# Moving one scale of the first tile from VectorE to ScalarE in a row normalization

## The chip, the cores and the metric

The kernel runs on one core of one Trainium2 chip. The metric is device time in microseconds (us) of one execution. Six runs of the kernel before and six of the changed one were taken in turn; a profile of one execution of each is read beside them. All runs are at a granted clock of 1.0.

## The reference

Each of 1024 rows of 4096 fp32 numbers is divided by its Euclidean norm.

```python
def reference(x, axis, eps):            # x: [1024, 4096] fp32, axis -1, eps 1e-12
    norm = np.sqrt(np.sum(x ** 2, axis=axis, keepdims=True) + eps)
    return (x / norm).astype(np.float32)
```

Every element is read once and written once: 16.78 MB in, 16.78 MB out.

## The kernel before

There are two tiles. A tile holds 512 rows: 128 partitions with R = 4 rows of 4096 elements each, 64 KB per partition and 8.39 MB in all. Both loads are issued at the start, on SyncE's DMA queue. For each tile, VectorE squares and sums row 3, ScalarE squares and sums rows 0, 1 and 2; ScalarE takes the root, VectorE the reciprocal; VectorE scales all four rows in place. Then one store sends the tile out on the same queue.

```python
    def scale(self, r):
        self.nc.vector.tensor_scalar_mul(
            out=self.x[:, r], in0=self.x[:, r], scalar1=self.rstd[:, r : r + 1]
        )
# ... (pools, constants)
    for i in range(n_tiles):
        g = RowGroups(nc, io, stats, scratch, D, R, eps_t)
        load = nc.sync.dma_start(out=g.flat(), in_=x_t[i])
        # ...
    for i, g in enumerate(groups):
        g.square_dve(R - 1)
        g.square_act(0)
        g.norm(0)
        g.scale(0)
        g.square_act(1)
        g.norm(1)
        g.norm(R - 1)
        g.scale(1)
        g.scale(R - 1)
        g.square_act(2)
        g.norm(2)
        g.scale(2)
        store = nc.sync.dma_start(out=out_t[i], in_=g.flat())
```

## Time and profile before

| | before |
|---|---|
| time, median of the first 3 runs | 82.73 us (82.72 to 83.13) |
| time, median of all 6 runs of the comparison | 82.97 us (82.72 to 83.13) |
| span of the profile | 81.1 us |
| VectorE / ScalarE busy | 28.6 us (35%) / 26.4 us (33%) |
| DMA queue, share of 16 engines' span | 97.1% |
| store 0 issued / tile 1's squares start / store 1 issued | 37.88 / 41.91 / 57.27 us |

Two rows of the groups of instructions matter for the change: the second holds the scale that moves, and the first ScalarE's squares, from which the length of the new Copy can be judged. The columns are line, engine, operation, output and input with shapes and count; then busy us and the mean ns of one; then the idle time before them and what ended it.

```profile
L33 ACT ACTIVATE sq_act<-xt 128x4096 f32<-128x4096 f32 x6 | 21.6, 3608 | 26.5 <-DMA xt<-in_x_dram 26.5
L64 DVE TENSOR_SCALAR xt<-xt,rstd 128x4096 f32<-128x4096 f32 x8 | 18.8, 2353 | 0.3
```

Until their last instructions the engines are idle mostly because they wait for loads (26.5 us on ScalarE, 25.0 us on VectorE). The queue row and the windows that the prediction shows say the same from the other side: the DMA engines are what is full.

### The profile page before, as it was taken

How to read it: one execution, taken by the hardware profiler on the slowest of the kernel's cores; microseconds unless marked ns; L12 is line 12 of the kernel's file. 1: busy time of each engine (PE TensorE's matmuls, PEld its weight loads, DVE VectorE, ACT ScalarE, POOL GpSimd, SP SyncE). 2: the span in 40 equal slices, each digit the busy share in tenths (PEclk: the TensorE clock that was granted, in tenths of full speed). 3: DMA queues.
4: the chain of work that ended last, by engine and by line, in shares of the span. 5: the costliest groups of instructions: out<-in, count | busy, mean ns of one | idle time of the engine just before them, and what ended most of it. 6: DMA issues, size and time to landing. Idle time of an engine off the chain costs nothing.

```text
span 81.1 us, 93 instructions
## 1 busy us (share of the span) xinstructions
DVE 28.6 (35%) x21; ACT 26.4 (33%) x22; POOL 0.2 (0%) x4
## 2 busy tenths in 40 slices
DVE  0000000000199599976039995999200000000000
ACT  6000000000199999930039999950000000000000
POOL 0000000000000000000000000000000000000000
DMA  9099999299999759999099995899998399998390
GB/s 517 0 517 517 517 517 485 129 420 517 517 517 485 323 226 517 517 517 517 0 517 517 517 452 226 355 517 517 517 485 388 162 517 517 517 517 388 162 485 0
DMA packets 577, 33.55 MB, mean 414 GB/s; under 512 B 65, under 2 KB 65, under 8 KB 65
## 3 DMA queue, kind: packets, MB, share of 16 engines
q1 hardware_dynamic: 576, 33.55, 97.1%
q14 instruction: 1, 0.00, 0.0%
HBM read 16.78 MB, written 16.78 MB: 414 GB/s over the span
## 4 chain that ended last, share of the span: by engine, by line
DMA 51%; ACT 10%; DVE 9%; issue 0%
DMA xt<-in_x_dram 51%; ACT sq_act L33 9%; DVE xt L64 9%; ACT rstd L53 1%; DVE rstd L59 0%
## 5 line engine op out<-in xcount | busy, mean ns | idle before, releaser
L33 ACT ACTIVATE sq_act<-xt 128x4096 f32<-128x4096 f32 x6 | 21.6, 3608 | 26.5 <-DMA xt<-in_x_dram 26.5
L64 DVE TENSOR_SCALAR xt<-xt,rstd 128x4096 f32<-128x4096 f32 x8 | 18.8, 2353 | 0.3
L42 DVE SCALAR_TENSOR_TENSOR sq_dve<-xt 128x4096 f32<-128x4096 f32 x2 | 8.9, 4426 | 25.0 <-DMA xt<-in_x_dram 25.0
L53 ACT ACTIVATE rstd<-ssq,eps_t 128x1 f32<-128x1 f32 x8 | 2.1, 288 | 0.1
L59 DVE RECIPROCAL rstd<-rstd 128x1 f32<-128x1 f32 x8 | 1.3, 159 | 2.4 <-ACT rstd L53 2.4
L33 ACT ACT_TABLE_LOAD x1 | 1.3, 1283 | 0.8 <-PEq L220 0.8
L53 ACT ACT_TABLE_LOAD x1 | 1.3, 1283 | 0.0
L33 ACT ACTIVATION_READ_ACCUMULATOR sq_act<-xt 128x1 f32 x6 | 1.1, 186 | 0.0
L176 DVE MEMSET eps_t<- 128x1 f32 x1 | 0.1, 59 | 0.9 <-PEq L220 0.9
L42 DVE DVE_READ_ACCUMULATOR sq_dve<-xt 128x1 f32 x2 | 0.2, 83 | 0.0
L220 POOL MEMSET const-uint8-127<- 128x1 uint8 x1 | 0.1, 102 | 0.0
L220 POOL MEMSET const-bfloat16-1.0<- 128x1 bf16 x1 | 0.1, 101 | 0.0
L220 POOL MEMSET const-float32-0.0<- 128x1 f32 x1 | 0.1, 98 | 0.2 <-issue 0.2
L220 POOL MEMSET const-float32-1.0<- 128x1 f32 x1 | 0.1, 98 | 0.0
## 6 DMA issues: line engine op xcount, KB each, us to landing
xt<-in_x_dram SPq DMA_DIRECT2D x2, 31.5
out_dram<-xt SPq DMA_DIRECT2D x2, 23.3
```

Source lines behind the costliest of these rows:

```text
L33: self.nc.scalar.activation(out=sq_a, in_=self.x[:, r], func=ACT_F.Square, accum_out=self.ssq[:, r : r + 1],)
L42: self.nc.vector.scalar_tensor_tensor(out=sq_v, in0=self.x[:, r], scalar=1.0, in1=self.x[:, r], op0=ALU.mult, op1=ALU.mult, accum_out=self ...
L53: self.nc.scalar.activation(out=self.rstd[:, r : r + n], in_=self.ssq[:, r : r + n], func=ACT_F.Sqrt, bias=self.eps_t,)
L59: self.nc.vector.reciprocal(out=self.rstd[:, r : r + n], in_=self.rstd[:, r : r + n])
L64: self.nc.vector.tensor_scalar_mul(out=self.x[:, r], in0=self.x[:, r], scalar1=self.rstd[:, r : r + 1])
L176: nc.vector.memset(eps_t, eps)
L220: nc = _bacc.Bacc("TRN2", target_bir_lowering=False, num_devices=1)
```

## The change

The intent is to relieve VectorE at the end of tile 0: its last scale there becomes a Copy with a per-row scale on ScalarE, which has nothing else to do until load 1 lands. Tile 1 is left alone, because there the last scale is followed by the last store and VectorE is the quicker engine.

```diff
+    def scale_act(self, r):
+        self.nc.scalar.activation(
+            out=self.x[:, r],
+            in_=self.x[:, r],
+            func=ACT_F.Copy,
+            scale=self.rstd[:, r : r + 1],
+        )
 ...
-        g.scale(2)
+        if i < n_tiles - 1:
+            g.scale_act(2)
+        else:
+            g.scale(2)
         store = nc.sync.dma_start(out=out_t[i], in_=g.flat())
```

## The prediction

> **What bounds the kernel now.** I read the busy table first: VectorE (DVE) is busy 35% of the span and ScalarE (ACT) 33%, so neither engine fills it. The slices, the packet line and the queue row come next.
>
> ```profile
> DMA  9099999299999759999099995899998399998390
> ...
> DMA packets 577, 33.55 MB, mean 414 GB/s; under 512 B 65, under 2 KB 65, under 8 KB 65
> ...
> q1 hardware_dynamic: 576, 33.55, 97.1%
> ```
>
> The one queue that carries both loads and both stores occupies the 16 DMA engines for 97.1% of the span. The single 0s between 9s in the slices are no holes: a packet is booked, with its bytes and its whole time, where it starts, and all 16 engines start their packets almost together. Each of the four transfers is 8.39 MB, 128 packets of 64 KB, so eight per engine. The windows of busy time, cut to fit the rounds of packets, show how long one lasts (DMA share times the length of the window, for 16 packets) and when it starts (columns: window, length, DVE, ACT, POOL, clock, DMA share, GB/s):
>
> ```profile
> 1.00:1.60 0.60, 0.00 (x0) 0.60 (x1) 0.00 (x0) 1.00 5.17 1748
> ...
> 35.60:36.10 0.50, 0.50 (x1) 0.00 (x0) 0.00 (x0) 1.00 4.88 2097
> 36.10:38.00 1.90, 1.75 (x1) 0.00 (x0) 0.00 (x0) 1.00 0.00 0
> 38.00:38.50 0.50, 0.00 (x0) 0.00 (x0) 0.00 (x0) 1.00 5.84 2097
> 38.50:40.80 2.30, 0.00 (x0) 0.00 (x0) 0.00 (x0) 1.00 0.00 0
> 40.80:41.60 0.80, 0.00 (x0) 0.00 (x0) 0.00 (x0) 1.00 2.84 1229
> ```
>
> 2097 GB/s for 0.50 us is 1.05 MB, 16 packets. A packet of the next to last load round took 4.88 x 0.50 = 2.44 us; the very first round took 5.17 x 0.60 = 3.10 us[...]. The last load round starts in 38.00 to 38.50 and takes 5.84 x 0.50 = 2.92 us, so it ends near 41.2 on average, and there the next 16 packets start (1229 GB/s for 0.80 us is 15 of them). Those are the first packets of store 0. The engines have no hole at this hand-over; only that last load round is 0.5 us longer than the usual 2.42, a fact I come back to. Four transfers of eight rounds are 32 x 2.42 = 77.4 us; with 1.0 us until the first packet, 0.7 us extra in the first round, 0.5 us at the hand-over, 0.1 us elsewhere and roughly 1 us for receipts and the closing barrier this gives the 81.1 us of the span. Bandwidth, not arithmetic, sets the end.
>
> The timeline shows when store 0 was ready, and the DMA queue's own waits what it stood behind:
>
> ```profile
> 34.98 0.29 ACT L53 ACTIVATE rstd<-ssq,eps_t 128x1 f32<-128x1 f32 x1
> 35.30 0.16 DVE L59 RECIPROCAL rstd<-rstd 128x1 f32<-128x1 f32 x1 [0.57 <-ACT rstd L53]
> 35.50 2.35 DVE L64 TENSOR_SCALAR xt<-xt,rstd 128x4096 f32<-128x4096 f32 x1
> 37.88 0.35 SPq L202 DMA_DIRECT2D out_dram<-xt  x1
> 41.91 3.62 ACT L33 ACTIVATE sq_act<-xt 128x4096 f32<-128x4096 f32 x1 [6.64 <-DMA xt<-in_x_dram]
> 41.91 4.43 DVE L42 SCALAR_TENSOR_TENSOR sq_dve<-xt 128x4096 f32<-128x4096 f32 x1 [4.06 <-DMA xt<-in_x_dram]
> ...
> SPq L202 <- DVE xt L64: 31.3, 2, 15.9
> SPq L234 <- DMA out_dram<-xt: 22.5, 2, 19.3
> ```
>
> The scale to be changed is the row at 35.50. Store 0 is issued at 37.88, but its packets start only from 40.8 on. Both compute engines then sit idle until 41.91, when load 1 has landed. The queue waits up to 15.9 us for the scales, yet the DMA engines are never empty meanwhile: such a wait is one of the issuing queue, not of the transfers. The chain of work that ended last, as printed, stops at the last scale (54.89); the 23 us after it are store 0's rest and store 1.
>
> **What the Trainium skill says.** ScalarE: Activation LUTs, section What ACT_TABLE_LOAD costs: an ACTIVATE with immediate scale and bias takes 186 ns plus 0.833 ns per element, and each [128,1] operand adds about 93 ns. The trace agrees: the squares of 4096 elements mean 3608 ns, the formula 3598. The same page, section Table sets: cheap functions, copy among them, are in every set, so Copy between Sqrt and Square should switch no table; in the trace Square already follows Sqrt without a second switch, and the changed program's list of ScalarE instructions has no added load. VectorE: DVE Perf Modes, section The perf-mode tier table: fp32 tensor_scalar from SBUF runs at twice the base rate; the trace has 2353 ns for 4096 elements, 1.74 elements per ns, so it does. DMA: Bandwidth & Descriptors, section Queues, rings and completion order: on each DMA engine descriptors are consumed in ring order. Store 0 starting only as load 1's last round ends agrees.
>
> **The change part by part.** The listing of both programs' instructions says: on VectorE one scale of tile 0 goes and nothing else moves; on ScalarE one Copy comes between the last square root of tile 0 and the first square of tile 1; on the queue, store 0 now waits for ScalarE. Tile 1 keeps all its work.
>
> Removed: 2.35 us of VectorE (35.50 to 37.85). Behind it VectorE has only the wait until 41.91, so this frees nothing: its idle time before tile 1 grows from 4.06 to about 6.6 us.
>
> Added: one ACTIVATE of 4096 elements with a [128,1] scale. My estimate from the skill's figures is 3598 + 93 = 3.69 us; from the measured squares it would be at least 3.60. ScalarE is free from 35.27, but the reciprocal it needs ends at 35.46, so it starts at about 35.50 and ends at about 39.19. ScalarE's next work starts at 41.91, so 2.7 us remain and no tile 1 work is pushed.
>
> Moved: the issue of store 0. Before, it came 0.03 us after the scale's end (35.50 + 2.35 = 37.85, issue at 37.88). Now it is 39.19 + 0.03 = 39.22, which is 1.34 us later.
>
> What that is worth depends on the hand-over. Load 0 was issued at 0.00 and its first packets started in 1.0 to 1.6, so I take 1.0 to 1.6 us from issue to first packet. Store 0's packets could then start at 40.2 to 40.8. Before, the engines came free for them from about 40.8 to 41.6. So the later issue still comes some 0.6 to 0.8 us ahead, where it was about 2 us ahead. On the path: 0. In the sum: minus 2.35 off the path, plus 3.69 off the path, 1.34 later into a slack of about 2.0. The load of tile 1, its arithmetic and the issue of store 1 at 57.27 stay where they are, and store 1 again waits in its ring behind store 0, which goes on until near 60.5.
>
> **The rivals.** *Rival 1: the slack is not there.* The last load round is 0.5 us long already. If this comes from store 0's descriptors arriving too late for the engines to look ahead to, the issue time is on the path now, and a delay of 1.34 us goes through partly or wholly: up to 82.73 + 1.34 = 84.07 us, 1.6% more. Even if the engines want the descriptors only one path filling (3.10 - 2.42 = 0.68 us) ahead of the data, then 0.6 to 0.8 us of lead is just enough, and without the long round, with engines free from 40.5, a few tenths would show. Against it speaks the hand-over from store 0 to store 1: store 1 is issued at 57.27, its descriptors arrive at 58.3 to 58.9, when the last round of store 0 is already running (it starts in 57.7 to 58.5), and that round is not longer (3.02 x 0.80 = 2.42 us for 16 packets). The long round may so belong to turning from loads to stores. I give 20% to a loss of 0.1 to 0.7 us and 12% to one nearer 1.3.
>
> *Rival 2: VectorE's relief helps.* Its idle time turns into an earlier end only if something of tile 1 could start earlier. Both first squares of tile 1 wait for the load at 41.91, so this yields 0, 82.7 us. Some gain could come only from the hand-over itself: if a later issue takes the extra 0.5 us out of the last load round, 82.3 us. I give 5% to that.
>
> *Rival 3: ScalarE becomes the bound.* It would have to be busy past 41.91, that is, the Copy would have to last 6.4 us, or switch tables twice (2 x 1.28 us, the rows of its table loads) and still end at 41.8. Neither fits the list of instructions; it would cost a few tenths at most, 83 us.
>
> **Range and chances.** The most likely result is no change, 82.73, with run-to-run scatter of 82.72 to 83.13 in the runs before. Weighing 63% at about 0, 20% at +0.4, 12% at +1.3 and 5% at -0.4 gives +0.2; the middle of the outcomes lies nearer zero, so I say 82.85 us. The range of 82.4 to 83.9 leaves out the corner of each rival. Faster by 2% would need 1.65 us, more than the hand-over has to give; slower by 2% would need 1.65 us also, above the full 1.34. Chances: faster 0.01, same 0.96, slower 0.03.
>
> **What would show each step.** Right: a Copy row of 3.6 to 3.7 us on ScalarE at 35.5, store 0 issued near 39.2, tile 1's squares still at 41.9 and the queue's share still near 97%. The hand-over is settled by when store 0's first packets start: 40.8 to 41.6 as before means hidden. If they start later by most of 1.34 us, or the last load round grows beyond 2.92 us, the slack step was wrong. A table load beside the Copy, or tile 1's squares later than 41.9, would make the ScalarE step wrong.

## The result, and the profile after

| | before | after |
|---|---|---|
| median of 6 runs | 82.97 us (82.72 to 83.13) | 82.53 us (82.44 to 82.70) |
| ratio after / before | | 0.9953 (95% interval 0.9930 to 0.9975) |

A ratio here is the mean time of one kernel's runs over the mean of the other's of the same rounds, so it is not quite the ratio of the medians. As predicted, 82.53 lies in the range. But the interval excludes 1: the kernel is 0.44 us faster by the medians, although the prediction said that nothing on the path would move.

The page of the kernel after, its packet line, its queue row and the row of the new instruction:

```profile
DMA packets 576, 33.55 MB, mean 416 GB/s; under 512 B 64, under 2 KB 64, under 8 KB 64
...
q1 hardware_dynamic: 576, 33.55, 97.0%
...
L69 ACT ACTIVATE xt<-xt,rstd 128x4096 f32<-128x4096 f32 x1 | 3.7, 3708 | 0.2 <-DVE rstd L59 0.2
```

The same bytes, the same share of the queue, a little more GB/s, and a Copy of 3708 ns without a table load. The timeline of the kernel after (start us, length us, engine, line, operation; idle time before it and what ended it in brackets):

```profile
35.48 3.71 ACT L69 ACTIVATE xt<-xt,rstd 128x4096 f32<-128x4096 f32 x1 [0.23 <-DVE rstd L59]
39.21 17.74 SPq L213 DMA_DIRECT2D out_dram<-xt  x2
41.25 3.62 ACT L33 ACTIVATE sq_act<-xt 128x4096 f32<-128x4096 f32 x1 [2.06 <-DMA xt<-in_x_dram]
41.25 4.43 DVE L42 SCALAR_TENSOR_TENSOR sq_dve<-xt 128x4096 f32<-128x4096 f32 x1 [5.81 <-DMA xt<-in_x_dram]
```

Store 0 is issued 1.33 us later (39.21 against 37.88), as worked out (1.34). Yet load 1 has landed 0.66 us *earlier* (41.25 against 41.91), and nothing in the change touches the load. The windows of the kernel after, cut at the rounds of packets, show where this comes from (columns: window, length, VectorE, ScalarE and GpSimd busy, clock, DMA share, GB/s; the share times the length is the mean time of a packet when all 16 start in the window):

```profile
35.50:36.10 0.60, 0.00 (x0) 0.60 (x1) 0.00 (x0) 1.00 4.03 1748
...
37.90:38.50 0.60, 0.00 (x0) 0.60 (x1) 0.00 (x0) 1.00 4.03 1748
38.50:40.50 2.00, 0.00 (x0) 0.69 (x1) 0.00 (x0) 1.00 0.00 0
40.50:41.05 0.55, 0.00 (x0) 0.00 (x0) 0.00 (x0) 1.00 4.47 1907
```

The last load round (37.90 to 38.50) takes 4.03 x 0.60 = 2.42 us, the usual length, where it took 2.92 before. The next 16 packets, store 0's first, start from 40.5 on. By the single packet records each engine now stands empty for 0.10 to 0.25 us, 0.18 us on average, between its last load packet and its first store packet; before there was no such hole.

The sum, from the packet records averaged over the 16 engines: the last load round is 0.50 us shorter; the three rounds before it, which were 0.13 us too long in the profile of before, are normal; the first round began and ran 0.10 us later; the hole costs 0.18 us; the 16 store rounds are together 0.13 us longer. That is -0.50 - 0.13 + 0.10 + 0.18 + 0.13 = -0.22 us. The end is set by the slowest of the 16 engines, not by the mean. The ends of the last packets lay 0.74 us apart before and lie 0.48 us apart after, so the slowest ends 0.43 us earlier (79.80 against 80.23), and the span falls from 81.1 to 80.7.

### The profile page after: what moved, and what is told of

It is laid out like the page before. It is cut to its first block, busy times and chain, and to the rows that moved or that the text cites. A ratio compares the mean times of both kernels' runs of the same rounds, so it can differ in the third digit from the quotient of the medians.

```text
span 80.7 us, 93 instructions
## 1 busy us (share of the span) xinstructions
DVE 26.2 (33%) x20; ACT 30.1 (37%) x23; POOL 0.2 (0%) x4
## 4 chain that ended last, share of the span: by engine, by line
DMA 50%; ACT 10%; DVE 9%; issue 0%
DMA xt<-in_x_dram 50%; ACT sq_act L33 9%; DVE xt L64 9%; ACT rstd L53 1%; DVE rstd L59 0%
## 5 line engine op out<-in xcount | busy, mean ns | idle before, releaser
L64 DVE TENSOR_SCALAR xt<-xt,rstd 128x4096 f32<-128x4096 f32 x7 | 16.5, 2353 | 0.2
L69 ACT ACTIVATE xt<-xt,rstd 128x4096 f32<-128x4096 f32 x1 | 3.7, 3708 | 0.2 <-DVE rstd L59 0.2
```

The costliest lines, as they stand in the source:

```text
L64: self.nc.vector.tensor_scalar_mul(out=self.x[:, r], in0=self.x[:, r], scalar1=self.rstd[:, r : r + 1])
L69: self.nc.scalar.activation(out=self.x[:, r], in_=self.x[:, r], func=ACT_F.Copy, scale=self.rstd[:, r : r + 1],)
```

## The experiments

The first theory (A) after the result: a store that is queued while a load still runs lengthens the load's last round, so the gain comes from the later issue of store 0 and from nothing else. The rivals: (B) the long last round was an accident of one profile; (C) the engine matters, for example because VectorE's scale disturbs the loads' writes and ScalarE's does not. Each run was timed in 5 rounds beside the kernel before. All results but one were correct.

| run | store 0 issued | last load round | hole | first store round | median, us | ratio to before (95%) |
|---|---|---|---|---|---|---|
| e5_early | 34.74 | 3.68 | 0 | 2.42 | 83.55 | 1.0084 (1.0067 to 1.0100) |
| e4_split_2048 | 37.47 | 3.18 | 0 | 2.42 | 83.04 | 1.0019 (0.9992 to 1.0045) |
| e1_before_again | 37.74 | 3.18 | 0 | 2.42 | 82.90 | 0.9994 (0.9965 to 1.0024) |
| kernel before | 37.88 | 2.92 | 0 | 2.42 | 82.97 | |
| e10_split_3072 | 38.41 | 2.50 | 0 | 2.42 | 82.45 | 0.9953 (0.9929 to 0.9977) |
| e9_split_3328 | 38.55 | 2.44 | 0 | 2.42 | 82.31 | 0.9935 (0.9908 to 0.9962) |
| e6_late_1024 | 38.61 | 2.43 | 0 | 2.42 | 82.19 | 0.9920 (0.9905 to 0.9935) |
| e7_late_1536 | 38.91 | 2.42 | 0.07 | 2.43 | 82.25 | 0.9926 (0.9911 to 0.9941) |
| e3_dve_late | 39.04 | 2.42 | 0.14 | 2.45 | 82.33 | 0.9929 (0.9905 to 0.9953) |
| e2_after_again | 39.12 | 2.42 | 0.13 | 2.44 | 82.44 | 0.9942 (0.9918 to 0.9966) |
| kernel after | 39.21 | 2.42 | 0.18 | 2.45 | 82.53 | 0.9953 (0.9930 to 0.9975) |
| e8_late_4096 | 40.28 | 2.42 | 0.63 | 2.46 | 82.73 | 0.9982 (0.9962 to 1.0001) |
| e11_act_queue | 38.03 (other queue) | 2.62 | 0 | 3.17 | 83.14 | 1.0035 (1.0013 to 1.0057) |

All columns in us; rounds and holes are means over the 16 engines from the packet records of one profile of each kernel. Runs e1 to e4, e5 to e8 and e9 to e11 were made in three groups on three different chips, each with its own runs of the kernel before (medians 82.88, 82.86 and 82.95 us), to which the ratios refer. The ratios are the safe comparison between groups; the kernel before was profiled again only in the first, so the last load rounds are compared across chips.

**e1_before_again.** No edit: the kernel before.

> The kernel before, unchanged, as a null test of the timing and as a second profile of the hand-over from load 1 to store 0. Theory A (store 0's descriptors reach the rings while load 1's last round still runs, and this lengthens that round): the last load round is again about 2.9 us against 2.42, store 0's issue at 37.9, load 1 landed at 41.9, time 82.7 to 83.1, ratio 1.000. Theory B (the long round and the slightly long rounds before it were an accident of the one profile): last load round 2.42 in this profile. The 0.06 us by which the rounds starting at 31 to 36 us were longer in the first profile should vary from run to run under both, as the instructions up to 35.5 us are the same in both kernels.

Measured: ratio 0.9994, and the long last round is there again. The window of that round in this profile:

```profile
37.90:38.40 0.50, 0.00 (x0) 0.00 (x0) 0.00 (x0) 1.00 6.35 2097
```

6.35 x 0.50 = 3.18 us, even longer than the 2.92 of the first profile. Theory B falls. What does vary from run to run is the other surplus: the three rounds before the last one were 0.13 us too long in the first profile and 0.03 us in this one, although the program is the same. That part of the first profile explains nothing.

**e2_after_again.** No edit: the kernel after.

> The changed kernel once more, on the same chip as the others. Theory A: last load round 2.42 us, a hole of about 0.2 us before store 0's first packets, load 1 landed at 41.25, time 82.5, ratio 0.995. Theory B: may go either way, ratio between 0.995 and 1.000.

Measured: ratio 0.9942, last load round 2.42 us, hole 0.13 us, tile 1's squares at 41.12. The result repeats.

**e3_dve_late.** All scales stay on VectorE; store 0 is delayed by a multiplication by 1.0.

```diff
         g.scale(2)
+        if i < n_tiles - 1:
+            g.times_one(2, 2048)   # vector.tensor_scalar_mul of x[:, 2, :2048] by 1.0, in place
         store = nc.sync.dma_start(out=out_t[i], in_=g.flat())
```

> All scales on VectorE as before; behind the last scale of tile 0 VectorE multiplies half of that row by 1.0 (2048 elements, about 1.3 us), so that store 0 is issued near 39.2 us as in the changed kernel, with no work moved to ScalarE. Theory A (the issue time alone does it): last load round 2.42, small hole, load 1 landed at 41.2, ratio 0.995, although the kernel does more work. Theory C (the engine does it: VectorE's scale slows the loads' last rounds, ScalarE's does not): last load round stays about 2.9 or grows, ratio 1.000 or up to 1.003.

The timeline, and then the window of the last load round:

```profile
37.79 1.23 DVE L69 TENSOR_SCALAR xt<-xt 128x2048 f32<-128x2048 f32 x1
39.04 0.35 SPq L209 DMA_DIRECT2D out_dram<-xt  x1
```

```profile
37.80:38.40 0.60, 0.60 (x1) 0.00 (x0) 0.00 (x0) 1.00 4.03 1748
```

The kernel does everything that the kernel before does and 1.23 us of useless VectorE work on top, and it is faster than it: ratio 0.9929. The last load round is 4.03 x 0.60 = 2.42 us. Theory C falls: ScalarE has no part in the gain. Moving the scale there helped because it was slower.

**e4_split_2048.** The last scale of tile 0 is shared between the two engines, so ScalarE takes part but the store is issued early.

```diff
-        g.scale(2)
+        if i < n_tiles - 1:
+            g.scale_split(2, 2048)   # ScalarE Copy of x[:, 2, :2048], VectorE x[:, 2, 2048:]
+        else:
+            g.scale(2)
```

> The last scale of tile 0 is shared: ScalarE does 2048 elements, VectorE the other 2048, side by side. ScalarE takes part, but store 0 is issued at about 37.5 us, earlier than in the kernel before. Theory A: last load round about 2.9 us, load 1 landed at 41.9, ratio 1.000. Theory C: somewhere between the two kernels, last load round 2.4 to 2.7, ratio 0.995 to 0.998.

The timeline:

```profile
35.44 2.00 ACT L69 ACTIVATE xt<-xt,rstd 128x2048 f32<-128x2048 f32 x1 [0.23 <-DVE rstd L59]
...
37.47 0.35 SPq L216 DMA_DIRECT2D out_dram<-xt  x1
```

The tile is ready sooner than in either kernel, by a better use of both engines, and the time is 83.04, ratio 1.0019. The last load round is 3.18 us (about 2.9 was expected). This and e3 together separate the two: the time follows the issue of store 0, not the engine.

**e5_early.** The last scale of tile 0 is left out, so the result is wrong.

```diff
-        g.scale(2)
+        if i == n_tiles - 1:
+            g.scale(2)
```

> Wrong result on purpose: the last scale of tile 0 is left out (a quarter of tile 0's output stays unscaled), so store 0 is issued at about 34.9 us, three us before the kernel before and some 5 us before load 1 ends. Theory A1 (the queued store lengthens the load round in which the queue turns from load to store, whenever it was queued): the last load round is again 2.9 to 3.2 us, the rounds before it 2.42, ratio 1.000. Theory A2 (the arrival of the descriptors itself disturbs the round that is then running): the round that starts at 35.5 us is lengthened, the last one is 2.42, ratio 1.000. If neither is longer, ratio 0.993.

The timeline, and then the windows of the last two load rounds:

```profile
34.74 0.35 SPq L203 DMA_DIRECT2D out_dram<-xt  x1
```

```profile
35.30:36.10 0.80, 0.15 (x1) 0.00 (x0) 0.00 (x0) 1.00 3.02 1311
...
37.70:38.50 0.80, 0.00 (x0) 0.00 (x0) 0.00 (x0) 1.00 4.60 1311
```

The store is issued about 0.6 us before the next to last load round starts, so its descriptors arrive while that round runs, if they take the 1.0 to 1.6 us that lie between issue and first packet at the program's start (an estimate; no view shows their arrival). That round takes 3.02 x 0.80 = 2.42 us and is untouched. The last one takes 4.60 x 0.80 = 3.68 us. So the runs speak for the load round behind which the store stands (theory A1), and against the arrival of the descriptors as such (A2), as far as that estimate goes. The expectation missed the size: I wrote 2.9 to 3.2 us and a ratio of 1.000 and got 3.68 and 1.0084. The longest wait in the queue has the highest cost: less work and an earlier store gave the slowest of all these kernels.

**e6_late_1024, e7_late_1536, e8_late_4096.** As e3, with another number of elements multiplied by 1.0.

```diff
-            g.times_one(2, 2048)
+            g.times_one(2, 1024)     # e6; 1536 in e7, 4096 in e8
```

> As the delayed kernel with all scales on VectorE, but with 1024 elements multiplied by 1.0 instead of 2048: store 0 issued near 38.45 us. Its first packets could start at about 39.9 to 40.3, ahead of the load's natural end at 40.3 to 40.8. If the cost of the turn falls gradually with a later issue, the last load round is between 2.5 and 2.9 and the ratio near 0.996. If it is all or nothing, either 2.9 or more and 1.000, or 2.42 with no hole and a ratio of about 0.991.

> 1536 elements: store 0 issued near 38.75 us, its first packets possible at 40.2 to 40.6, about when the engines come free. Under theory A this is close to the best place: last load round 2.42 to 2.6, hole below 0.1 us, ratio 0.991 to 0.994. If an early arrival of only part of the descriptors already costs the full turn, last load round 2.7 or more and ratio 0.997 to 1.000.

> 4096 elements: store 0 issued near 40.2 us, 1.1 us later than the delayed kernel. Theory A: last load round 2.42, and the hole grows by the whole further delay to about 1.25 us, so the time is near 83.4 us, ratio 1.006. This is what was left over of the slack in the prediction: it says how late is too late.

The windows of e6, at the last load round and the first store round:

```profile
37.80:38.50 0.70, 0.67 (x2) 0.00 (x0) 0.00 (x0) 1.00 3.47 1498
38.50:40.30 1.80, 0.08 (x1) 0.00 (x0) 0.00 (x0) 1.00 0.00 0
40.30:40.90 0.60, 0.00 (x0) 0.00 (x0) 0.00 (x0) 1.00 4.04 1748
```

Both rounds last 2.42 us (3.47 x 0.70 and 4.04 x 0.60), and the packet records have no hole. With store 0 issued at 38.61 the queue turns from load to store without loss, and the ratio is 0.9920. Issued 0.30 us later (e7) some engines already stand empty for up to 0.24 us.

e8 is a miss in size. I expected a hole of 1.25 us and a ratio of 1.006; the hole is 0.63 us and the ratio 0.9982. The windows show why:

```profile
38.60:41.10 2.50, 1.65 (x1) 0.00 (x0) 0.00 (x0) 1.00 0.00 0
41.10:41.30 0.20, 0.00 (x0) 0.00 (x0) 0.00 (x0) 1.00 12.28 5243
```

Issued at 40.28, all first packets start from 41.13 to 41.27, so 0.85 to 0.99 us after the issue, with the engines empty or nearly so. In the kernel after it took 1.32 to 1.81 us. I had added the delay to that longer time.

**e9_split_3328, e10_split_3072.** As e4 with the cut moved, so that no work is wasted and store 0 is issued near the best place.

```diff
-            g.scale_split(2, 2048)
+            g.scale_split(2, 3328)   # e9; 3072 in e10
```

> A candidate that wastes no work: the last scale of tile 0 is shared, ScalarE 3328 elements (estimate from the measured 2.00 us for 2048 and 3.71 us for 4096: about 3.07 us), VectorE 768, so that store 0 is issued near 38.6 us, where the kernel with 1024 elements times 1.0 had neither a longer last load round nor a hole. Theory A: last load round 2.42 to 2.45, hole below 0.03 us, load 1 landed at 41.2, ratio 0.991 to 0.993. If the work on the engines mattered and not the issue time: ratio between 0.994 and 1.000.

> The same with ScalarE 3072 elements, store 0 issued near 38.35 us, between 37.9 (last load round 0.50 to 0.76 us longer) and 38.6 (not longer). If the cost falls in a straight line from 0.50 at 37.9 to 0 at 38.6, the last load round is about 2.6 us and the ratio 0.994 to 0.996; if there is a threshold, 2.42 and 0.992 or 2.9 and 1.000.

The timeline of e9, and then the window of its last load round:

```profile
35.46 3.07 ACT L69 ACTIVATE xt<-xt,rstd 128x3328 f32<-128x3328 f32 x1 [0.23 <-DVE rstd L59]
...
38.55 0.35 SPq L216 DMA_DIRECT2D out_dram<-xt  x1
```

```profile
37.70:38.50 0.80, 0.00 (x0) 0.80 (x1) 0.00 (x0) 1.00 3.05 1311
```

3.05 x 0.80 = 2.44 us, no hole, ratio 0.9935. The estimate of 3.07 us for the Copy holds to two digits. e9 is faster than the kernel before, and at 82.31 us it is nominally ahead of the kernel after, but the intervals overlap widely, so that order is not shown. e10, issued at 38.41, has 2.50 us: 0.08 us longer, less than the straight line of the expectation gives for 38.41 (0.14 us). The fall is steep, and it is not the same on all engines: by the single packets 10 of the 16 last load packets take the usual 2.42 to 2.43 us, and the three that start last take 2.51 to 2.87. So the mean falls because fewer engines pay. (The profile of e10 is that of its slowest run, 82.66 us.)

**e11_act_queue.** The kernel before, but store 0 is issued on ScalarE's own queue.

```diff
-        store = nc.sync.dma_start(out=out_t[i], in_=g.flat())
+        queue = nc.scalar if i < n_tiles - 1 else nc.sync
+        store = queue.dma_start(out=out_t[i], in_=g.flat())
```

> The kernel before, but store 0 is issued by ScalarE on its own queue, still behind VectorE's last scale at 37.9 us. Theory A3 (what costs is a store standing in the same ring behind the load): load and store packets now share the engines from about 39 us, load 1 lands later, at 42 to 44 us, but the engines lose nothing: all 32 rounds fit without the extra 0.5 us, ratio 0.993 to 0.996. Theory A4 (what costs is any store waiting beside a load that still runs): 0.5 us or more is lost all the same, ratio 1.000 to 1.010.

The windows of the last load round and of store 0's first round:

```profile
37.80:38.60 0.80, 0.20 (x1) 0.00 (x0) 0.00 (x0) 1.00 3.28 1311
...
40.40:41.40 1.00, 0.00 (x0) 0.00 (x0) 0.00 (x0) 1.00 3.18 1049
```

The last load round is 3.28 x 0.80 = 2.62 us, the first store round 3.18 x 1.00 = 3.18 us: 0.2 us and 0.76 us over the usual 2.42. The loss has moved, for the most part, into another round, and the time is 83.14 us, not shorter. Theory A4 fits and A3 does not: a ring of its own does not save the turn. Load 1 landed at 41.65. The run does not show whether packets of two rings would alternate: by the packet records every engine had started its last load packet by 38.59 (the first at 37.81), 0.56 us after the store's issue and sooner than any first packet followed its issue in these runs (0.85 us in e8), so no load packets were left for the store's to mix with.

## Why the prediction was right or wrong, point by point

**What bounds the kernel.** Right. The queue stayed at 97.0%, and taking 2.35 us off VectorE or adding 1.23 us to it (e3) has no effect of its own.

**Removed and added work.** Right. The Copy took 3708 ns, 18 ns more than the estimate of 3.69 us from the Trainium skill's page ScalarE: Activation LUTs, section What ACT_TABLE_LOAD costs; there was no table load beside it; store 0 was issued at 39.21 against the 39.22 worked out. Tile 1 lost nothing on ScalarE.

**"So the later issue still comes some 0.6 to 0.8 us ahead ... On the path: 0."** This step failed, twice in opposite directions. First, the slack was not there. I took the 1.0 to 1.6 us between issue and first packet from the start of the program, and the time at which the engines come free from the stretched round (40.8 to 41.6). In the kernel after it was 1.32 to 1.81 us, and the engines came free at 40.33 to 40.92; the first packets started at 40.53 to 41.02, on average 0.18 us late on each engine. Second, and larger, I took an early issue to be free. It was not: standing in the queue behind the load cost the load's last round 0.50 us in the profile before, and the later issue took this back. In the sum above these two make -0.50 + 0.18 = -0.32 us, and its other terms bring it to -0.22. That the medians differ by 0.44 us agrees with the 0.43 us by which the slowest engine ended earlier in this pair of profiles, and is not split further. The stated 82.85 us leaned to slower (82.73 before), and the kernel became faster; that 82.53 still lies in the range is in part luck, since e6 and e7, whose stores meet no stretched round and hardly a hole, came to 82.19 and 82.25, below its lower end of 82.4.

**Rival 1.** Its observation was the right one, its sign for the larger effect was wrong. I had seen that the last load round was 0.5 us too long, and took it for a sign that the store's descriptors came too late. The store came too early: e5 made the store 3.1 us earlier and the round grew to 3.68 us, e6 made it 0.7 us later and the round was normal. What did come of Rival 1 is its side remark that without the long round, with the engines free from 40.5, "a few tenths would show": that is the hole of 0.18 us. The sentence within it that "the long round may so belong to turning from loads to stores" is what the runs support: at the turns from load 0 to load 1 and from store 0 to store 1 the last rounds measure 2.42 us, although store 1 too was issued just before the last round in front of it began (57.27 against 57.7 to 58.5).

**Rival 2.** Its second half, "if a later issue takes the extra 0.5 us out of the last load round, 82.3 us", is what happened, and it had been given 5%. The 82.53 measured is 0.2 us more, about as much as the hole. That a hole costs time is shown within one group: e6 with none took 82.19 us, e8 with 0.63 us took 82.73. The first half, that tile 1's squares are fixed at 41.91, was wrong as well: they follow the load, and started at 41.25; store 1 was issued at 56.61 instead of 57.27, which is of no use to it, since it waits behind store 0.

**Rival 3.** Right to be set aside: ScalarE was free 2.06 us before its next work.

**What stays open.** Why a waiting store lengthens the load's last packets is not settled. The Trainium skill's page DMA: Bandwidth & Descriptors, section Two DMAs through the same engine are not ordered, states that descriptors start in order but are pipelined, and that an engine's read and write sides are separate queues. A store whose read side starts while the load's writes are under way would fit e5 (only the last load round suffers), e11 (a second ring moves the loss and does not save it) and the same-direction turns (no cost). It is an argument; no run here looks into an engine, and none has a turn from stores to loads. Nor is it shown how far the cost grows beyond the 1.26 us of e5.

## What to carry to other kernels

On a kernel bound by DMA, look at the packets where the queue turns from loads to stores: neither the waits of the compute engines nor the share of the queue (97.1% and 97.0%) singles out a packet that takes 3.2 us instead of 2.4. A store made ready earlier was slower here; the best issue time of those tried lay about 2.6 us before load 1 had landed (38.61 against 41.24 in e6; e3, e7 and e9 are not set apart from it by their intervals), with a stretched load round on the early side and empty engines on the late side, and the whole effect is about 1%. Test such a reason by shifting the time alone, with useless work on the old engine, before crediting the engine.

## What the Trainium skill lacked or had wrong

- DMA: Bandwidth & Descriptors, section Rules for kernel authors, advises to issue a DMA early, compute, and wait late. It does not say that a store waiting behind a running load lengthens the load's last packets: 64 KB packets took 2.92 to 3.18 us with the store issued at 37.5 to 37.9 us, 3.68 us with 34.7, and 2.42 to 2.44 us from 38.55 on. Between two loads or two stores they took 2.42 to 2.44.
- The same page, section Issuing engines are not separate DMA queues, states that DMAs of different issuing engines run on the same engines and interleave. It does not say what a store on the other queue costs a load that is ending: issued on ScalarE's queue at 38.03 us, the store started as the last load round ended; that round took 2.62 us, the store's first 3.17, and the kernel 83.14 us against 82.95. Interleaving itself is not tested here (see e11).
- The same page, section Specifications, gives about 0.6 us of first-byte latency for the hardware path. Counted from the start of the issuing instruction, 0.85 to 0.99 us lay before the first packets on engines that were empty or nearly so (e8), 1.0 to 1.6 us at program start, and 1.32 to 1.81 us when the load was just ending (the kernel after). The issuing instruction itself takes 0.35 us, and counted from its end e8 has 0.50 to 0.64 us, so the page's figure is not wrong for the empty engines; it does not say from where it counts, and no page gives this spread.
